# First products of every stage interleaved, and the residual, merged and last gate tiles turned by VectorE and DMA instead of TensorE

## The chip, the cores and the metric

The kernel runs on one core of a Trainium2 chip. The metric is the device time of one launch, in microseconds (us). Of three timed runs the median counts; beside them stands one profiled run, whose trace the rows below come from.

## What the kernel computes

One block of a network on 256 tokens of width 2048, in float32. Cut to what matters:

```python
h = rms_norm(x, ffn1_norm)
x = x + 0.5 * ((silu(h @ w1_gate) * (h @ w1_up)) @ w1_down)      # D_FF = 5632
h = rms_norm(x, mix_norm)
proj = h @ w_in                                                  # 2048 -> 3072
y_a = s5_mixer(proj[:, :1024], ...)                              # diagonal state space, then a GLU
y_b = sgu_mixer(proj[:, 1024:], ...)                             # gated by a 128-token mixing
g_a, g_b = split(sigmoid(h @ w_gate + b_gate))
merged = g_a * (y_a @ w_branch_a) + g_b * (y_b @ w_branch_b)
x = x + merged @ w_out
h = rms_norm(x, ffn2_norm)
x = x + 0.5 * ((silu(h @ w2_gate) * (h @ w2_up)) @ w2_down)
out = rms_norm(x, final_norm)
```

## The kernel before

Tokens are the rows of every result: 256 tokens are two halves of 128 partitions, and a result tile is 128 x 2 x 512 in PSUM (`acc`, three buffers). The weights stream once: chunks of 128 x 2048 floats (1 MB) come from HBM on SyncE's queue into `raw`, ScalarE rounds a chunk to `whi`, VectorE takes the rest as `wlo = raw - whi`, and each product is the sum of three matmuls (hi x whi, hi x wlo, lo x whi). A chunk holds four k-steps of 512 columns, and a **step** is six matmuls of 512 columns: three for each token half. `job(lhs, kt, evac)` runs kt steps into one `acc` and then queues `evac`, which reads the result.

The program is written out by one counter of steps (`tick`). Before each step a tick runs the functions that were put there with `at(delta, fn)`, then the waiting evacuations, and, at the first step of a chunk, the split of the chunk two further on; fillers (the preparation of the S5 mixer, for instance) get their turns by a credit per tick. Each engine runs what it got in this order.

The left operand of a product must have its contraction index on the partitions, so every result that feeds a later product is turned. There are two ways in the kernel:

- `turned`: eight TensorE transposes of 128 x 128 into two PSUM tiles `q`, then `put`, which splits them into hi and lo on ScalarE and VectorE.
- `turned_dma`: two VectorE transposes of 32 x 32 blocks (128 x 512 each) into a tile `tt`, four DMAs on GpSimd's queue to a DRAM tile `turn` in runs of 32 floats, one DMA back into `w`, and `put` a fixed number of steps after the evacuation.

In each of the two feed-forward stages the 11 gate tiles are made in groups of 4, 4 and 3 (`GROUPS`); each group's down product follows it, over 16, 16 and 12 steps a tile and four tiles of 512 columns. All gate tiles but a group's last go through `turned_dma`; the group's last, the four tiles of x after each of the first two residual sums (`residual`), and the four merged tiles (`ba_evac`) go through `turned`. A stage's first product needs the last tile of the stage before at its step 12 of 16 (8 of 12).

Of the kernel before, what the change touches and what calls it, by code (L numbers as in the profile page):

```python
# [18 lines left out]
P = 128  # L19
# [11 lines left out]
GROUPS = (4, 4, 3)  # L31
# [19 lines left out]
def kernel(  # L51
# [57 lines left out]
    def add_ffn(wg, wu, wd, first):  # L109
        j, d = 0, 0  # L110
        for n in GROUPS:
            for _ in range(n):
                if j == 0 and first is not None:
                    add(first)
                else:
                    i = j - (first is not None)
                    add(wg, 4 * i, 4)
                    add(wu, 4 * i, 4)
                j += 1
            add(wd, d, 4 * n)  # L120
            d += 4 * n

    add_ffn(w1g, w1u, w1d, w1s)
    add(w_in)
# [7 lines left out]
    add(w_out)  # L132
    add_ffn(w2g, w2u, w2d, None)
# [115 lines left out]
    def split_gain(dst, src, g, k):  # L249
        act.activation(out=dst[:, 0, :], in_=src, func=AF.Copy, scale=g[:, k:k + 1])  # L250
        dve.scalar_tensor_tensor(out=dst[:, 1, :], in0=src, scalar=g[:, k:k + 1],
                                 in1=f(dst[:, 0, :]), op0=ALU.mult, op1=ALU.subtract)
# [10 lines left out]
    def turned_dma(src, pl, put, wait):  # L263
        tt = tmp()
        for h in range(2):
            dve.transpose(out=tt[:, h, :], in_=src[:, h, :])  # L266
        d = dr.tile([4, 32, 2, 4, P], F32, tag="turn", name="turn", bufs=2)
        dv = d.rearrange("b j h k (a i) -> a j (h k) b i", a=4)
        for a in range(4):
            pool.dma_start(out=dv[a], in_=tt[32 * a:32 * a + 32].rearrange("j h (k b i) -> j (h k) b i", k=4, b=4))  # L270
        w = pl.tile([P, 2, 4, P], F32, tag="tw", name="w")
        pool.dma_start(out=w.rearrange("p h k t -> p (h k t)"), in_=d.rearrange("b j h k t -> (b j) (h k t)"))

        def arrived():
            for h in range(2):
                put(slice(h * P, h * P + P), w[:, h])
        at(wait, arrived)
# [36 lines left out]
    def residual(hT, g, scale):  # L314
        def make(m):
            def put(b, q):
                for i in range(2):
                    k = 4 * m + 2 * b + i
                    split_gain(hT[:, k], q[:, i, :], g, k)

            def evac(acc):
# [3 lines left out]
                at(2, lambda: turned(x_sb, m * N, put))  # L325
# [5 lines left out]
    def ffn(hT, gp, last_down, begin=None, rates=None):  # L331
# [8 lines left out]
        def up_evac(gt, j, n):  # L340
            def put(b, q):
                split2(gt[:, 4 * j + 2 * b:4 * j + 2 * b + 2], q)

            def evac(acc):
# [13 lines left out]
        for i, n in enumerate(GROUPS):  # L358
# [3 lines left out]
            for j in range(n):  # L362
                if begin is not None and i == 0 and j == 0:
                    begin(gate_evac, up_evac(gt, j, n))
# [3 lines left out]
            if i == len(GROUPS) - 1:  # L368
                last_down(gt, 4 * n)
            else:  # L370
                for m in range(4):
                    job(gt, 4 * n, down(m))
# [461 lines left out]
    def down_mix(gt, kt):  # L834
# [4 lines left out]
        for m in range(4):  # L839
            job(gt, kt, mk(m))  # L840

    ffn(h1, gp, down_mix, begin, (0.3, 0.35, 0.35))
# [24 lines left out]
    def load_bias(i):  # L867
        b = ev.tile([P, N], F32, tag="bias", name="bias", bufs=2)
# [53 lines left out]
    job(h2, KD, gelu_to(v, 0))  # L922
    job(h2, KD, gelu_to(v, 1))
# [118 lines left out]
    def ba_evac(n):  # L1042
        def put(b, q):
            split2(mT[:, 4 * n + 2 * b:4 * n + 2 * b + 2], q)
# [11 lines left out]
    for m in range(4):  # L1056
        job(mT, KD, lambda acc, m=m: later["mk"](m)(acc))
        if m == 0:
            mxr.release()
            mxa.release()  # L1060
            h3p = tc.alloc_tile_pool(name="h3p", bufs=1)
            h3 = h3p.tile([P, KD, 2, T], F32R, name="h3")
            later["mk"] = residual(h3, g3, 1.0)
    gp2 = tc.alloc_tile_pool(name="gp2", bufs=1)

    def down_out(gt, kt):
# [19 lines left out]
        for m in range(3):  # L1086
            job(gt, kt, evac(m))
# [27 lines left out]
    ffn(h3, gp2, down_out)  # L1115
# [8 lines left out]
def _layout(inputs):  # L1124
# [14 lines left out]
    def down(w):  # L1139
        parts, r = [], 0  # L1140
        for n in GROUPS:
# [7 lines left out]
    def pairs(a):  # L1149
# [20 lines left out]
        'w1s': start, 'w1g': wide(wg[:, N:]), 'w1u': wide(wu[:, N:]), 'w1d': down(i['ffn1_w_down'][0]),  # L1170
# [11 lines left out]
        'w2g': wide(i['ffn2_w_gate'][0]), 'w2u': wide(i['ffn2_w_up'][0]), 'w2d': down(i['ffn2_w_down'][0]),  # L1182
# [23 lines left out]
```

## Time and profile before

| | us |
|---|---|
| three timed runs | 2028.51, 2028.75, 2030.27 (median 2028.75) |
| the profiled run's own time | 2029.23 |
| its span, first to last instruction | 2027.3 |
| TensorE (PE) busy | 2008.8 (99%) |
| VectorE (DVE) busy | 1145.8 (57%) |
| ScalarE (ACT) busy | 864.4 (43%) |
| GpSimd (POOL) busy | 144.9 (7%) |
| mean granted TensorE clock | 0.997 |

Busy time of TensorE is counted from modelled ends: two matmuls that overlap count once, so a share of 99% says that it hardly ever stood still, not how fast it worked. What a matmul costs is read from the distance between the starts of neighbours.

### The profile page before, as it was taken

To read this page: it belongs to the slowest core of one execution; us is meant where nothing else is said; L and a number is where in the kernel's file an instruction comes from. 1 tells how busy PE (TensorE), PEld (TensorE's weight loads), DVE (VectorE), ACT (ScalarE), POOL (GpSimd) and SP (SyncE) were. 2 spreads that over 40 slices of the span, in tenths; PEclk is the share of its full clock that TensorE was granted. 3 is DMA by queue.
4 is the path that set the end of the run, shared out by engine and by line. 5 is a ranking of instruction groups with operands and counts; after the bars stand their busy time and mean duration, and the time that the engine had idled before them with its cause. 6 is when DMAs were issued, how large, how long until landed. Compare 5 with 4: busy or idle time off the path is not lost.

```text
span 2027.3 us, 23118 instructions
## 1 busy us (share of the span) xinstructions
PE 2008.8 (99%) x9636; PEld 1660.9 (82%) x9636; DVE 1145.8 (57%) x1138; ACT 864.4 (43%) x709; POOL 144.9 (7%) x214
## 2 busy tenths in 40 slices
PE   9999999999999999999999999999999999999998
PEld 7888888888888888878888988888888888888886
DVE  5775555666664555556775565544554445544454
ACT  7544334444334454434434544534433343333343
POOL 0111002221010000011100000000000000000100
PEclk9999999999999999999999999999999999999999
DMA  8667666765666556556765454566655666555653
GB/s 314 229 229 251 229 237 227 239 227 201 217 234 210 182 182 216 199 184 245 240 223 202 185 187 171 198 213 218 218 187 189 217 217 209 189 202 194 224 207 125
DMA packets 71865, 428.97 MB, mean 212 GB/s; under 512 B 11552, under 2 KB 12208, under 8 KB 25936
## 3 DMA queue, kind: packets, MB, share of 16 engines
q1 hardware_dynamic: 53280, 378.56, 52.8%
q0 software_dynamic: 16032, 44.71, 7.7%
q10 hardware_dynamic: 2448, 4.22, 0.6%
q8 instruction: 75, 1.23, 0.2%
q14 instruction: 30, 0.25, 0.0%
HBM read 406.60 MB, written 20.84 MB: 211 GB/s over the span
## 4 chain that ended last, share of the span: by engine, by line
PE 97%; DVE 1%; DMA 1%; ACT 1%; issue 1%; SPq 0%; ACTq 0%
PE acc L218 31%; PE acc L220 31%; PE acc L219 31%; PE q L260 1%; DMA raw<-in_w1s_dram 1%; ACT whi L148 0%; DVE wlo L149 0%; PE q L609 0%; PE acc L236 0%; PE acc L235 0%; PE acc L234 0%; PE q L745 0%; PE q L702 0%; DVE r L671 0%; PE acc L1099 0%
## 5 line engine op out<-in xcount | busy, mean ns | idle before, releaser
L149 DVE TENSOR_TENSOR wlo<-raw,whi 128x2048 fp32r<-128x2048 f32 (+1 forms) x363 | 815.3, 2248 | 772.6 <-ACT whi L148 772.6
L148 ACT ACTIVATE whi<-raw 128x2048 fp32r<-128x2048 f32 (+1 forms) x363 | 682.6, 1882 | 920.3 <-PE acc L220 853.7
L218 PE MATMUL acc<-whi,h 128*128 128x512 f32 x1856 | 725.9, 391 | 0.8 <-ACT whi L148 0.8
L219 PE MATMUL acc<-wlo,h 128*128 128x512 f32 x1856 | 723.2, 390 | 1.1 <-DVE wlo L149 1.1
L220 PE MATMUL acc<-whi,h 128*128 128x512 f32 x1856 | 722.7, 389 | 0.0
L218 PEld LDWEIGHTS acc<-whi,h 128*128 128x128 f32 x1856 | 348.8, 188 | 74.7 <-ACT whi L148 1.4
L219 PEld LDWEIGHTS acc<-wlo,h 128*128 128x128 f32 x1856 | 348.7, 188 | 73.9 <-DVE wlo L149 2.5
L220 PEld LDWEIGHTS acc<-whi,h 128*128 128x128 f32 x1856 | 348.6, 188 | 72.5
L218 PE MATMUL acc<-whi,gt 128*128 128x512 f32 x680 | 266.6, 392 | 0.0
L220 PE MATMUL acc<-whi,gt 128*128 128x512 f32 x680 | 265.9, 391 | 0.0
L219 PE MATMUL acc<-wlo,gt 128*128 128x512 f32 x680 | 264.8, 389 | 0.0
L220 PEld LDWEIGHTS acc<-whi,gt 128*128 128x128 f32 x680 | 127.7, 188 | 27.5
L219 PEld LDWEIGHTS acc<-wlo,gt 128*128 128x128 f32 x680 | 127.7, 188 | 27.4
L218 PEld LDWEIGHTS acc<-whi,gt 128*128 128x128 f32 x680 | 127.7, 188 | 26.4
L270 POOL DMA_DIRECT2D turn<-t x64 | 63.5, 999 | 931.2 <-DVE t L266 931.2
L337 ACT ACTIVATE t<-acc,rc 128x512 f32<-128x512 f32 x44 | 27.9, 685 | 63.4 <-PE acc L220 63.4
L218 PE MATMUL acc<-whi,mT 128*128 128x512 f32 x128 | 50.2, 392 | 0.0
L312 DVE SCALAR_TENSOR_TENSOR x_sb<-acc,x_sb 128x1024 f32<-128x1024 f32 x27 | 33.1, 1225 | 29.7 <-PE acc L220 29.7
L220 PE MATMUL acc<-whi,mT 128*128 128x512 f32 x128 | 49.8, 389 | 0.0
L219 PE MATMUL acc<-wlo,mT 128*128 128x512 f32 x128 | 49.8, 389 | 0.0
L291 ACT ACTIVATE junk<-x_sb 128x512 bf16<-128x512 f32 x32 | 20.2, 630 | 56.9 <-DVE x_sb L312 51.6
L347 DVE SCALAR_TENSOR_TENSOR t<-acc,rc,t 128x512 f32<-128x512 f32 x44 | 30.9, 745 | 16.8 <-PE acc L220 16.8
(205 smaller groups left out, 1086.3 us busy)
## 6 DMA issues: line engine op xcount, KB each, us to landing
raw<-in_w1d_dram SPq DMA_DIRECT2D x44, 1024.0 KB, 4.9
raw<-in_w2g_dram SPq DMA_DIRECT2D x44, 1024.0 KB, 4.8
raw<-in_w2u_dram SPq DMA_DIRECT2D x44, 1024.0 KB, 5.5
raw<-in_w2d_dram SPq DMA_DIRECT2D x44, 1024.0 KB, 4.8
raw<-in_w1g_dram SPq DMA_DIRECT2D x40, 1024.0 KB, 5.0
raw<-in_w1u_dram SPq DMA_DIRECT2D x40, 1024.0 KB, 5.9
raw<-in_w_in_dram SPq DMA_DIRECT2D x24, 1024.0 KB, 4.8
raw<-in_w_gb_dram SPq DMA_DIRECT2D x16, 1024.0 KB, 5.0
```

The lines of the kernel that those rows point to most:

```text
L148: act.activation(out=hi[:, s], in_=r[:, s], func=AF.Copy)
L149: dve.tensor_tensor(out=lo[:, s], in0=r[:, s], in1=f(hi[:, s]), op=ALU.subtract)
L218: pe.matmul(acc[:, h, :], lhsT=lhs[:, k, 0, t], rhs=hi, start=first, stop=False)
L219: pe.matmul(acc[:, h, :], lhsT=lhs[:, k, 0, t], rhs=lo, start=False, stop=False)
L220: pe.matmul(acc[:, h, :], lhsT=lhs[:, k, 1, t], rhs=hi, start=False, stop=last)
L260: pe.transpose(q[:, i, h * P:h * P + P], src[:, h, c:c + P], ident)
L270: pool.dma_start(out=dv[a], in_=tt[32 * a:32 * a + 32].rearrange("j h (k b i) -> j (h k) b i", k=4, b=4))
L291: act.activation(out=j, in_=x_sb[:, h, m * N:m * N + N], func=AF.Square, accum_out=ssq[:, h, m:m + 1])
L312: dve.scalar_tensor_tensor(out=xs, in0=acc, scalar=scale, in1=xs, op0=ALU.mult, op1=ALU.add)
L337: act.activation(out=s[:, h, :], in_=acc[:, h, :], func=AF.Silu, scale=rc(h))
L347: dve.scalar_tensor_tensor(out=s[:, h, :], in0=acc[:, h, :], scalar=rc(h), in1=s[:, h, :], op0=ALU.mult, op1=ALU.mult)
```

## The change

`braid` takes two or three products at once: it runs all but the last four steps of each, one product after the other, and then the last four steps of each. It is used for the first two products (three where they have 12 steps) of each down product, of `w_in`, of `w_out` and of the second feed-forward stage, and the weight chunks are put in the same order. A stage's last tile is so first needed at step 24. With that, the residual tiles, the merged tiles and the last gate tile of each group go through `turned_dma` too, with waits of 18, 16 and 17 steps; the other gate tiles wait 24 steps instead of 26. The tile `w` becomes two halves, each loaded by a DMA of its own, which share two buffers with the bias tiles. The residual's split works on pieces of 128 x 128 instead of 128 x 256. The first feed-forward stage's groups become 3, 4, 4. `turned` stays in two places, the SGU's tiles (`ub`) and the S5's input tiles (`ua_evac`).

```diff
-GROUPS = (4, 4, 3)
+GROUPS1 = (3, 4, 4)
+GROUPS2 = (4, 4, 3)
...
+    def braid(jobs, between=None):
+        accs = [new_acc() for _ in jobs]
+        for (lhs, kt, _), acc in zip(jobs, accs):
+            for k in range(kt - 4):
+                step(acc, lhs, k, k == 0, False)
+        if between:
+            between()
+        for (lhs, kt, evac), acc in zip(jobs, accs):
+            for k in range(kt - 4, kt):
+                step(acc, lhs, k, False, k == kt - 1)
+            pend.append(lambda evac=evac, acc=acc: evac(acc))
...
-        w = pl.tile([P, 2, 4, P], F32, tag="tw", name="w")
-        pool.dma_start(out=w.rearrange("p h k t -> p (h k t)"), in_=d.rearrange("b j h k t -> (b j) (h k t)"))
-
-        def arrived():
+        w = []
+        for h in range(2):
+            w.append(half_tile("w").rearrange("p (k t) -> p k t", k=4))
+            pool.dma_start(out=w[h].rearrange("p k t -> p (k t)"),
+                           in_=d[:, :, h].rearrange("b j k t -> (b j) (k t)"))
+        at(wait, lambda: put(w))
...
     def residual(hT, g, scale):
         def make(m):
-            def put(b, q):
-                for i in range(2):
-                    k = 4 * m + 2 * b + i
-                    split_gain(hT[:, k], q[:, i, :], g, k)
+            def put(w):
+                for i in range(4):
+                    k = 4 * m + i
+                    for h in range(2):
+                        split_gain(hT[:, k, :, h * P:h * P + P], w[h][:, i], g, k)
 
             def evac(acc):
                 add_residual(acc, m, scale)
                 for h in range(2):
                     square(m, h)
-                at(2, lambda: turned(x_sb, m * N, put))
+                turned_dma(x_sb[:, :, m * N:m * N + N], put, 18)
...
-                if j < n - 1:
-                    turned_dma(s, gp, lambda c, w: split2(gt[:, 4 * j:4 * j + 4], w, c), 26)
-                else:
-                    at(2, lambda: turned(s, 0, put))
+                turned_dma(s, split_turned(gt[:, 4 * j:4 * j + 4]), 24 if j < n - 1 else 17)
...
+    def downs(gt, kt, evacs):
+        b = strands(kt // 4)
+        braid([(gt, kt, e) for e in evacs[:b]])
+        for e in evacs[b:]:
+            job(gt, kt, e)
...
-    job(h2, KD, gelu_to(v, 0))
-    job(h2, KD, gelu_to(v, 1))
+    braid([(h2, KD, gelu_to(v, 0)), (h2, KD, gelu_to(v, 1))])
...
         def evac(acc):
-            t = tmp()
-            dve.tensor_tensor(out=t, in0=acc, in1=cols(ga, n), op=ALU.mult)
+            t = cols(ga, n)
+            dve.tensor_tensor(out=t, in0=acc, in1=t, op=ALU.mult)
             dve.tensor_tensor(out=t, in0=t, in1=cols(mb, n), op=ALU.add)
-            at(2, lambda: turned(t, 0, put))
+            turned_dma(t, split_turned(mT[:, 4 * n:4 * n + 4]), 16)
...
+    braid([(mT, KD, out_evac(m)) for m in range(2)], open_h3)
+    for m in (2, 3):
+        job(mT, KD, out_evac(m))
...
-        for m in range(3):
-            job(gt, kt, evac(m))
+        braid([(gt, kt, evac(m)) for m in range(3)])
```

What the change moves is shown at three places. The first is TensorE at the start of the output product `w_out`, whose left operand is the merged tile `mT`. Before, the last merged tile `t` is turned there, after the first two steps of the first product (`acc_8487`):

```order
L220 MATMUL acc_8487<-whi_8415,mT_8191 128x512
L260 MATMUL q_8509<-ident_80,t_8488 128x128 x4
L260 MATMUL q_8516<-ident_80,t_8488 128x128 x4
L218 MATMUL acc_8487<-whi_8415,mT_8191 128x512
L219 MATMUL acc_8487<-wlo_8416,mT_8191 128x512
```

With the change, after step 12 of the first product (`acc_8544`) the second product (`acc_8545`) begins, and no transpose stands among the steps:

```order
L237 MATMUL acc_8544<-whi_8566,mT_8253 128x512
L238 MATMUL acc_8544<-wlo_8567,mT_8253 128x512
L239 MATMUL acc_8544<-whi_8566,mT_8253 128x512
L237 MATMUL acc_8545<-whi_8596,mT_8253 128x512
L238 MATMUL acc_8545<-wlo_8597,mT_8253 128x512
L239 MATMUL acc_8545<-whi_8596,mT_8253 128x512
```

The eight transposes are gone from TensorE's row of work, and the four last steps of the first product stand behind twelve of the second.

The second place is VectorE at the same stage. Before, a merged tile is made (`t` from `acc` and the gate `ga`, plus `mb`), the next chunk's `wlo` follows, and then the split of the tile from PSUM (`q`):

```order
L1048 TENSOR_TENSOR t<-acc,ga 128x1024
L1049 TENSOR_TENSOR t<-t,mb 128x1024
L149 TENSOR_TENSOR wlo<-raw,whi 128x2048
L247 TENSOR_TENSOR mT<-q,mT 128x2x256 x2
L149 TENSOR_TENSOR wlo<-raw,whi 128x2048
```

With the change, from the second tile's making on: its block transposes, two chunks, the split of the first tile, and the start of the third tile's making:

```order
L1085 TENSOR_TENSOR ga<-acc,ga 128x2x512
L1086 TENSOR_TENSOR ga<-ga,mb 128x2x512
L300 STREAM_TRANSPOSE t<-ga 128x512 x2
L168 TENSOR_TENSOR wlo<-raw,whi 128x2048 x2
L278 TENSOR_TENSOR mT<-w,mT 128x4x128 x2
L1085 TENSOR_TENSOR ga<-acc,ga 128x2x512
```

Two block transposes a tile are new on VectorE; the split reads a tile `w` that a DMA brings, and stands four chunks behind its tile's making where it stood one behind.

The third place is ScalarE where the first feed-forward stage ends and `w_in` begins: `junk,ssq` are the squares of an x tile, `h` its split. Before:

```order
L291 ACTIVATE junk,ssq<-x_sb 128x512 x2
L148 ACTIVATE whi<-raw 128x2048
L250 ACTIVATE h_4783<-q,vec_sb 128x256 x4
L280 ACT_TABLE_LOAD
L280 ACTIVATE rc<-sm,eps_t 128x2
L148 ACTIVATE whi<-raw 128x2048 x3
```

With the change the last tile's split stands four chunks later, and the one before it lies where the last one's was:

```order
L330 ACTIVATE junk,ssq<-x_sb 128x512 x2
L167 ACTIVATE whi<-raw 128x2048
L281 ACTIVATE h_4683<-w,vec_sb 128x128 x8
L319 ACT_TABLE_LOAD
L319 ACTIVATE rc<-sm,eps_t 128x2
L167 ACTIVATE whi<-raw 128x2048 x4
L281 ACTIVATE h_4683<-w,vec_sb 128x128 x8
L167 ACTIVATE whi<-raw 128x2048 x2
```

Each split of `h` waits there for a DMA's tile `w`, with the following chunks' `whi` behind it in the same queue.

## Rows read from the trace of the kernel before

**Rows 1.** The page: busy time of each engine, and the chain of work that ended last, by engine and by line.

```profile
PE 2008.8 (99%) x9636; PEld 1660.9 (82%) x9636; DVE 1145.8 (57%) x1138; ACT 864.4 (43%) x709; POOL 144.9 (7%) x214
PE 97%; DVE 1%; DMA 1%; ACT 1%; issue 1%; SPq 0%; ACTq 0%
```

**Rows 2.** Who TensorE's matmuls waited for: line waited at, releaser, us in total, times, longest.

```profile
PE q L260 <- DVE u_all L934: 4.6, 1, 4.6
...
PE acc L219 <- DVE wlo L149: 1.1, 3, 0.6
```

**Rows 3.** The transposes of `turned` (L260), by what they read: count, and duration of one in ns (shortest, median, longest).

```profile
L260 PE MATMUL q<-ident,t x96: 270/273/446, 185.6 to 1955.8; 128*128 128x128 f32 x96
...
L260 PE MATMUL q<-ident,x_sb x64: 271/272/273, 695.2 to 1300.2; 128*128 128x128 f32 x64
```

**Rows 4.** TensorE in order of time around one call of `turned` on a residual tile, and then around one on a merged tile: start, us, instruction.

```profile
695.02 0.39 PE L220 MATMUL acc<-whi,gt 128*128 128x512 f32 x1
695.25 1.03 PE L260 MATMUL q<-ident,x_sb 128*128 128x128 f32 x8
696.04 0.48 PE L218 MATMUL acc<-whi,gt 128*128 128x512 f32 x1
...
696.82 0.39 PE L218 MATMUL acc<-whi,gt 128*128 128x512 f32 x1
...
1184.44 0.40 PE L220 MATMUL acc<-whi,yas 128*128 128x512 f32 x1
1184.75 1.06 PE L260 MATMUL q<-ident,t 128*128 128x128 f32 x8
1185.57 0.47 PE L218 MATMUL acc<-whi,yas 128*128 128x512 f32 x1
...
1186.34 0.39 PE L218 MATMUL acc<-whi,yas 128*128 128x512 f32 x1
```

**Rows 5.** ScalarE, then VectorE, in order of time over two chunks of the second feed-forward stage: splits of weights (L148, L149), the split of a gate tile that `turned_dma` brought (L246, L247), and the evacuation of the next one (L347, L266). In brackets the engine's idle time before, and what ended it.

```profile
1417.52 1.92 ACT L148 ACTIVATE whi<-raw 128x2048 fp32r<-128x2048 f32 x1 [3.52 <-PE acc L220]
1419.35 1.13 ACT L246 ACTIVATE gt<-w 128x512 fp32r<-128x512 f32 x2
1422.96 1.92 ACT L148 ACTIVATE whi<-raw 128x2048 fp32r<-128x2048 f32 x1 [2.48 <-PE acc L220]
...
1419.47 2.29 DVE L149 TENSOR_TENSOR wlo<-raw,whi 128x2048 fp32r<-128x2048 f32 x1 [3.15 <-ACT whi L148]
1421.68 1.29 DVE L247 TENSOR_TENSOR gt<-w,gt 128x512 fp32r<-128x512 f32 x2
...
1428.40 1.41 DVE L347 SCALAR_TENSOR_TENSOR t<-acc,rc,t 128x512 f32<-128x512 f32 x2 [1.20 <-PE acc L220]
1429.73 1.29 DVE L266 STREAM_TRANSPOSE t<-t 128x512 f32<-128x512 f32 x2
```

**Rows 6.** GpSimd's queue in order of time: the four issues to `turn` and the issue of `w`, for the call whose evacuation ends rows 5, for one late in the second feed-forward stage and for one early in the first. Below them the time from issue to landing of the DMAs of L270 and of L272 (shortest, median, longest).

```profile
1431.32 3.96 POOL L270 DMA_DIRECT2D turn<-t  x4 [32.96 <-DVE t L266]
...
1868.37 3.96 POOL L270 DMA_DIRECT2D turn<-t  x4 [164.02 <-DVE t L266]
1878.23 0.56 POOL L272 DMA_DIRECT2D w<-turn  x1 [5.90 <-DMA turn<-t]
...
100.13 3.95 POOL L270 DMA_DIRECT2D turn<-t  x4 [34.68 <-DVE t L266]
111.84 0.56 POOL L272 DMA_DIRECT2D w<-turn  x1 [7.76 <-DMA turn<-t]
...
DMA to landing us min/median/max: 3.3/5.8/8.1
...
DMA to landing us min/median/max: 3.6/4.3/7.2
```

**Rows 7.** VectorE in order of time: four splits of 128 x 128 pieces in the SGU (L913); and the first half of a merged tile's making (L1048). Then ScalarE's and VectorE's split of residual tiles as they are (128 x 256), grouped by line: count, busy us, mean ns of one.

```profile
838.08 1.12 DVE L913 SCALAR_TENSOR_TENSOR ub<-q,bs_sb,ub 128x128 f32<-128x128 f32 x4
...
1170.19 1.23 DVE L1048 TENSOR_TENSOR t<-acc,ga 128x1024 f32<-128x1024 f32 x1 [1.20 <-PE acc L220]
...
L251 DVE SCALAR_TENSOR_TENSOR h<-q,vec_sb,h 128x256 fp32r<-128x256 f32 x32 | 14.7, 480 | 8.7 <-ACT h L250 8.7
L250 ACT ACTIVATE h<-q,vec_sb 128x256 fp32r<-128x256 f32 x32 | 14.1, 467 | 23.8 <-DVE h L251 23.8
```

**Rows 8.** VectorE in order of time in the last down product: the evacuation of the second tile (L312, L1073) and the `wlo` behind it, then the same of the third tile, and the two results that end the kernel (L1102).

```profile
1986.06 1.22 DVE L312 SCALAR_TENSOR_TENSOR x_sb<-acc,x_sb 128x1024 f32<-128x1024 f32 x1 [1.20 <-PE acc L220]
1987.32 1.29 DVE L1073 TENSOR_TENSOR fin<-x_sb,fin 128x512 f32<-128x512 f32 x2
1990.70 2.29 DVE L149 TENSOR_TENSOR wlo<-raw,whi 128x2048 fp32r<-128x2048 f32 x1 [2.08 <-ACT whi L148]
...
2010.54 0.69 DVE L1102 SCALAR_TENSOR_TENSOR x_sb<-acc,x_sb 128x512 f32<-128x512 f32 x1 [1.46 <-PE acc L1100]
...
2018.70 0.69 DVE L1102 SCALAR_TENSOR_TENSOR x_sb<-acc,x_sb 128x512 f32<-128x512 f32 x1 [4.43 <-PE acc L1100]
```

**Rows 9.** TensorE in order of time behind its longest wait: two neighbouring matmuls there; and the stretch of 8 us about them (us, busy PE, PEld, DVE, ACT, POOL, granted clock, DMA share, GB/s).

```profile
869.42 0.63 PE L219 MATMUL acc<-wlo,h 128*128 128x512 f32 x1
869.85 0.63 PE L220 MATMUL acc<-whi,h 128*128 128x512 f32 x1
...
864.00:872.00 8.00, 5.94 (x20) 4.96 (x21) 3.80 (x12) 0.00 (x0) 1.47 (x2) 0.57 0.59 200
```

More of the change, by code (lines that the diff above doesn't have):

```diff
@@ L107, in add, with braided, strands, add_ffn @@
         chunks.extend(w[i] for i in range(a, w.shape[0] if n is None else a + n))
-    def add_ffn(wg, wu, wd, first):
+    def braided(w, a, n, jobs):
+        for i in range(jobs):
+            add(w, a + n * i, n - 1)
+        for i in range(jobs):
+            add(w, a + n * i + n - 1, 1)
+    def strands(n):
+        return 2 if n == 4 else 3
+    def add_ffn(wg, wu, wd, groups, first):
         j, d = 0, 0
-        for n in GROUPS:
+        for n in groups:
             for _ in range(n):
-                if j == 0 and first is not None:
+                i = j - (first is not None)
+                if i < 0:
                     add(first)
+                elif j == 0:
+                    add(wg, 0, 3)
+                    add(wu, 0, 3)
+                    add(wg, 3, 1)
+                    add(wu, 3, 1)
                 else:
-                    i = j - (first is not None)
                     add(wg, 4 * i, 4)
@@ L261, in turned, with half_tile, turned_dma @@
             put(b, q)
-    def turned_dma(src, pl, put, wait):
+    def half_tile(name):
+        return ev.tile([P, N], F32, tag="half", name=name, bufs=2)
+    def turned_dma(src, put, wait):
         tt = tmp()
@@ L329, in residual, with ffn @@
         return make
-    def ffn(hT, gp, last_down, begin=None, rates=None):
+    def ffn(hT, gp, groups, last_down, begin=None, rates=None):
         state = {}
@@ L356, in down @@
             return lambda acc: add_residual(acc, m, 0.5)
-        for i, n in enumerate(GROUPS):
+        for i, n in enumerate(groups):
             gt = gp.tile([P, 16, 2, T], F32R, tag="gt", name="gt")
@@ L362, in ffn @@
             for j in range(n):
-                if begin is not None and i == 0 and j == 0:
-                    begin(gate_evac, up_evac(gt, j, n))
+                if i == 0 and j == 0:
+                    if begin is not None:
+                        begin(gate_evac, up_evac(gt, j, n))
+                    else:
+                        braid([(hT, KD, gate_evac), (hT, KD, up_evac(gt, j, n))])
                     continue
@@ L367, in ffn @@
                 job(hT, KD, up_evac(gt, j, n))
-            if i == len(GROUPS) - 1:
+            if i == len(groups) - 1:
                 last_down(gt, 4 * n)
             else:
-                for m in range(4):
-                    job(gt, 4 * n, down(m))
+                downs(gt, 4 * n, [down(m) for m in range(4)])
+    def downs(gt, kt, evacs):
[3 more added lines that the diff above has]
+            job(gt, kt, e)
     stash_e = dr.tile([2, 2, 4, NPAIR, 64], F32, name="stash_e")
@@ L838, in down_mix @@
         mk = residual(h2, g2, 0.5)
-        for m in range(4):
-            job(gt, kt, mk(m))
-    ffn(h1, gp, down_mix, begin, (0.3, 0.35, 0.35))
+        downs(gt, kt, [mk(m) for m in range(4)])
+    ffn(h1, gp, GROUPS1, down_mix, begin, (0.3, 0.35, 0.35))
     gp.release()
@@ L867, in load_bias @@
     def load_bias(i):
-        b = ev.tile([P, N], F32, tag="bias", name="bias", bufs=2)
+        b = half_tile("bias")
         act.dma_start(out=b, in_=bgr[i:i + 1, :].to_broadcast([P, N]))
@@ L1055, with out_evac, open_h3 @@
     later = {}
[L1056 to L1063, printed above, removed]
+    def out_evac(m):
+        return lambda acc: later["mk"](m)(acc)
+    def open_h3():
+        mxr.release()
+        mxa.release()
+        later["p"] = tc.alloc_tile_pool(name="h3p", bufs=1)
+        later["h3"] = later["p"].tile([P, KD, 2, T], F32R, name="h3")
+        later["mk"] = residual(later["h3"], g3, 1.0)
+    braid([(mT, KD, out_evac(m)) for m in range(2)], open_h3)
+    for m in (2, 3):
+        job(mT, KD, out_evac(m))
+    h3p, h3 = later["p"], later["h3"]
     gp2 = tc.alloc_tile_pool(name="gp2", bufs=1)
@@ L1137, in cols, with down @@
         return a.reshape(-1, P).T
-    def down(w):
+    def down(w, groups):
         parts, r = [], 0
-        for n in GROUPS:
+        for n in groups:
             parts.append(wide(w[r:r + n * N]))
```

36 lines of the change are left out of this document (19 added, 17 removed).

## The prediction, made blind

> **What bounds the kernel now.** I read the busy times and the chain first: TensorE is busy 99% of the span and makes 97% of the chain that ended last [rows 1]. Busy time can hide waits, so the table of waits came next: the matmuls of the products waited for weights about a microsecond in all, and the one long wait, 4.6 us, is for an S5 input tile that the change leaves alone [rows 2]. Then the pace in the timeline: neighbours start 0.23 us apart [rows 4], so a step of six matmuls takes 1.37 us and a chunk of four 5.47 us. ScalarE shows the same from the other side: its splits start 5.44 us apart, and its idle time ends when TensorE gives a weight buffer back [rows 5]. TensorE sets the pace; whatever leaves its queue comes off the time, as long as nothing new makes it wait.
>
> **What is removed.** A call of `turned` has eight transposes; 64 on `x_sb` and 96 on `t` [rows 3] are 8 calls and 12. The 8 on x go, and of the 12 all but the two of `ua_evac`: 6 on gate tiles and 4 on merged tiles. Together 18 calls, 144 transposes. What a call costs is the place that it takes in TensorE's row. On an x tile, four starts of ordinary matmuls later than 695.02 would be 695.94 and was 696.82: 0.88 us. On a merged tile, four starts after 1184.44 would be 1185.36 and was 1186.34: 0.98 us [rows 4]. With 0.88 for x and gate tiles: 14 x 0.88 + 4 x 0.98 = 16.2 us.
>
> The transposes' own durations say something else: 144 x 272 ns = 39.2 us [rows 3]. The Trainium skill ("TensorE: Matmul & The Clock Gate", part 4 on the PE-mode transpose) gives about 275 ns for such a transpose in a kernel's context; the trace agrees on the duration. By it the sum would be 39.6 us and the time 1989. But eight of them fill 1.03 us in the row, not 2.2 [rows 4]: they overlap, and the place taken counts.
>
> The reordering itself (braids, groups 3, 4, 4) adds and removes no matmul: nothing. It needs two or three `acc` at once, of three: the third is the last up tile's, read out at the braid's start and used 16 steps later.
>
> **What is added, and what hides it.** Per call: two block transposes on VectorE, 1.29 us [rows 5], about 6 us of GpSimd's issuing, and three DMA legs. In a chunk of 5.47 us VectorE has 2.29 us of `wlo`, ScalarE 1.92 of `whi` [rows 5]; both have room. A split of weights is done 4.24 us after its buffer comes free (1417.52 to 1421.76 [rows 5]) and is used two chunks, 10.9 us, later: 6.7 us of cover. This is what hides everything that is put in front of a split; gone, each us late costs TensorE one.
>
> The question is whether the tiles arrive. From the evacuation's start to the first issue on GpSimd it is 2.9 us [rows 5, 6]; from there to the issue of `w` 9.9 us, 11.7 in the slowest call shown; to the landing 4.3 (3.6 to 7.2) [rows 6]. Together 17.1 us, at most 21.8; the second half of `w` follows 0.56 us later. The waits are 16, 17, 18 and 24 steps: 21.9, 23.3, 24.7, 32.9 us. So `put` finds its tile there, and step 24, where the last tile of a stage is first read, is 32.9 us after its evacuation. Gate and x tiles: 0 us of stall.
>
> Three places are tighter.
>
> (a) *Two x tiles four steps apart.* Braided evacuations follow each other at 4 steps, and there are two halves of `w` only: GpSimd holds the second tile's `w` until the first tile's split has read its own. In the last down product of the first stage, with evacuations at steps 28 and 32, the first split is emitted at 46 and done at about 49 (16 pieces: on VectorE 8 x 0.28 = 2.2 us [rows 7]; on ScalarE no more than 8 x 0.467 = 3.7 [rows 7]). The second `w` is issued then and lands some 5 us later, near step 52.5. The second split stands at step 50, so ScalarE waits there and is free at about 54.5; the weights due at 52 are done by 57.6 instead of 55 and needed at 60. 3.3 us of cover are left: 0. With the slowest landing (7.2) 0.4 us are left: still 0.
>
> (b) *Merged tiles.* They come every 8 steps (10.96 us), with 16 steps' wait, and GpSimd needs 9.9 to 11.7 us from the first issue to `w`, plus 1.1 for its two issues. From the stage's start in us: tile 0 is ready to issue at 10.96 + 2 x 1.23 [rows 7] + 1.6 = 15.0, its `w` goes out at 25.3 (10.3, between the two calls) and lands at 29.6. Tile 1 follows on GpSimd at 26.4, `w` 36.7; tile 2 at 37.8, `w` 48.1, landed 52.4 and 53.0. VectorE ends the `wlo` before it at 53.6 and splits tile 2 by 54.9. The output product's first product reads it at its step 8, which is step 40 here: 54.8. Just in time: between 0 and, with 11.7 and 7.2 all along (`w` of tile 2 out at 52.3, landed 59.5 and 60.1), about 5.3 us of stall. I take 0.3, since the rows' usual times lie at that end.
>
> (c) *The end.* The last down product now has evacuations at steps 28, 32 and 36. Each keeps the next `wlo` back: 1986.06 to 1992.99, 6.9 us [rows 8] against 5.47 for a chunk. After two in a row `wlo` is done 13.9 us after step 28; the chunk is read 12 matmuls after step 36, at 13.7. Stall 0 to 0.3 us; I take 0.2. The third evacuation ends at 18.6, before the first half of the last tile at 19.1 (the halves end 8.16 us apart [rows 8]).
>
> S5's preparation gets 147 turns instead of 150 before the drain and ends before it; its places move, for which I allow 0, within 1 us either way.
>
> **The sum.** -16.2 + 0.3 + 0.2 = -15.7 us. The profiled run, 2029.23 us, would become 2013.5; it lies 0.48 above the median, so the median 2028.75 becomes **2013.0 us**.
>
> **The rivals.**
>
> *Merged tiles late* (b at its upper end). 5.3 us of stall, and a wait of that length has a price of its own: behind the wait of 4.6 us the granted clock's mean was 0.57, the lower level of 1.2 GHz, and matmuls started 0.43 us apart instead of 0.23, six of them: 1.2 us [rows 9]. 2013.0 - 0.3 + 6.5 = 2019.2. For it: GpSimd takes 11.0 to 12.8 us per tile and they come every 10.96. Against: no `w` came later than 21.8 us.
>
> *Slower: the splits wait for tiles at every place.* ScalarE works in order, and behind each `put` stand weights. If the way through DRAM took longer than wait plus cover less the split's own work (about 1.1 us for gate and merged tiles, 2.4 for x), that is 28.9, 27.5 and 29.0 us, each of the 18 calls would stop TensorE. The gain is eaten where 6(L - 28.9) + 4(L - 27.5) + 8(L - 29.0) = 16.2: at L = 29.5 us; at 32 it is 60.6 us of stalls and 2073. Against: 16 calls of before show 17 to 22 us, under the same stream of weights. The Trainium skill speaks for it: "VectorE: DVE Perf Modes", on the three transpose paths and the rules for authors, would have a 128 x 128 transpose done by TensorE where PSUM will do, and calls a plain strided DMA copy 19 times slower than the DMA transpose (1.31 us): an estimate from it is 25 us a block, eight to a call. No run here shows that: the trace has a whole call, 32 x 32 blocks already turned by VectorE, at about 17 us.
>
> *No change: TensorE's place is filled by waits.* If weights were the limit, the gaps would stay and the time with them, 2028.7. Against: a microsecond of waits for weights in the whole span [rows 2], ScalarE idle 3.5 us before each split [rows 5].
>
> **How the numbers follow.** Gain of 14 to 18 us: 0.80. Late merged tiles or several small stalls, 2015 to 2020: 0.13. No change: 0.03. Slower: 0.04. The likeliest case alone is 2011 to 2015: up to 0.2 us more a call and S5's 1 us below, the small stalls doubled above. The range, 2011 to 2019, takes in most of the second case. A change of 0.2%, 4 us, is about what a measurement of this kernel can tell from none; faster by more 0.93, within it 0.03, slower 0.04.
>
> **What would show it.** Right: transposes on `t` and `x_sb` down to 16, starts 0.23 us apart across the places where they were, no new releaser among TensorE's waits, `w` landing 16 to 22 us after the evacuation. (a) wrong: ScalarE's split `h<-w` in the waits with many us and `acc` waiting for `whi` or `wlo` behind it. (b) wrong: a wait of TensorE for `mT` at step 8 of the output product, and a stretch at half clock. (c) wrong: a wait for `wlo` in the last 25 us. The prediction fails if `w` takes more than 27 us, or if the long wait at the S5 input grows or goes.

## The result, and the profile after

The changed kernel takes 2014.57 us (median of four runs, 2013.46 to 2018.92), the kernel before 2028.63 beside it (four runs, 2028.26 to 2030.27): a ratio of 0.9933, 95% interval 0.9918 to 0.9948. That is 14.1 us less, where 15.7 were forecast (2013.0, range 2011 to 2019). The profiled run took 2014.35 us with a span of 2012.6, against 2027.3 before.

The page of the changed kernel, busy time and the chain that ended last, as in [rows 1]:

```profile
PE 1992.8 (99%) x9492; PEld 1646.2 (82%) x9492; DVE 1170.9 (58%) x1206; ACT 870.1 (43%) x741; POOL 245.2 (12%) x338
PE 95%; DMA 2%; DVE 1%; ACT 1%; issue 0%; POOL 0%; SPq 0%; ACTq 0%; POOLq 0%; DVEq 0%
```

TensorE has the 144 instructions less and still makes nearly the whole chain. GpSimd is busy 100 us more and VectorE 25 more, and they make no more than 1% of the chain each. What is left of the transposes on `t`, to be read beside [rows 3] (busy us, mean ns, then idle time before them and its cause):

```profile
L291 PE MATMUL q<-ident,t 128*128 128x128 f32 x16 | 2.9, 318 | 4.6 <-DVE u_all L974 4.6
```

The operand `x_sb` is gone and `t` is down from 96 to 16; the 16 transposes on the SGU's `ub`, which the change leaves alone, stay. TensorE's waits after, as in [rows 2] (us in total, times, longest):

```profile
PE q L291 <- DVE u_all L974: 4.6, 1, 4.6
...
PE q L948 <- DVE u_all L974: 1.2, 1, 1.2
PE acc L237 <- ACT mT L277: 1.2, 1, 1.2
```

The long wait at the S5 input is what it was. One releaser is new: `mT`, the merged tile. TensorE in order of time at that place, step 8 of the output product's first product, and below it ScalarE's split of the tile for which it waits:

```profile
1206.62 0.39 PE L239 MATMUL acc<-whi,mT 128*128 128x512 f32 x1
1208.19 0.50 PE L237 MATMUL acc<-whi,mT 128*128 128x512 f32 x1 [1.19 <-ACT mT L277]
...
1208.92 0.50 PE L239 MATMUL acc<-whi,mT 128*128 128x512 f32 x1
1209.54 0.50 PE L237 MATMUL acc<-whi,mT 128*128 128x512 f32 x1
...
1210.61 0.40 PE L237 MATMUL acc<-whi,mT 128*128 128x512 f32 x1
...
1207.51 0.63 ACT L277 ACTIVATE mT<-w 128x512 fp32r<-128x512 f32 x1 [3.99 <-DMA w<-turn]
1208.86 0.63 ACT L277 ACTIVATE mT<-w 128x512 fp32r<-128x512 f32 x1 [0.72 <-DMA w<-turn]
```

From 1206.62 to 1210.61 there are seven distances, 3.99 us; at the usual 0.23 they would be 1.60. So this place costs 2.4 us, the wait of 1.19 and the pieces about it, and ScalarE had stood still for the DMA of `w`. Why the tile is late shows in GpSimd's queue: the merged stage, then the first residual tiles of the stage behind it (an issue of four DMAs to `turn`, then the two of `w`; in brackets what GpSimd waited for):

```profile
1167.32 4.10 POOL L304 DMA_DIRECT2D turn<-t  x4 [103.35 <-DVE t L300]
1179.13 1.11 POOL L308 DMA_DIRECT2D w<-turn  x2 [7.71 <-DMA turn<-t]
1180.22 3.98 POOL L304 DMA_DIRECT2D turn<-t  x4
1192.17 1.10 POOL L308 DMA_DIRECT2D w<-turn  x2 [7.97 <-DMA turn<-t]
1193.27 3.99 POOL L304 DMA_DIRECT2D turn<-t  x4
1204.31 1.11 POOL L308 DMA_DIRECT2D w<-turn  x2 [7.05 <-DMA turn<-t]
...
1239.54 3.98 POOL L304 DMA_DIRECT2D turn<-t  x4 [21.66 <-DVE t L300]
1248.05 1.11 POOL L308 DMA_DIRECT2D w<-turn  x2 [4.54 <-DMA turn<-t]
1249.14 3.98 POOL L304 DMA_DIRECT2D turn<-t  x4
1264.82 1.10 POOL L308 DMA_DIRECT2D w<-turn  x2 [11.70 <-DVE h L282]
```

In the merged stage it is 11.8, 12.0 and 11.0 us from the first issue to that of `w`; the residual tile at 1239.54 needs 8.5 (the one behind it is held on purpose, until the first split has read its half of `w`). With 1.1 us for the issue of `w`, a tile takes GpSimd 12.7 us on the mean of these three, and the tiles come every 10.96: each stands in the queue for longer than the one before, and the third is the one TensorE waits for.

### The profile page after: what moved, and what is told of

It is laid out like the page before. It is cut to its first block, busy times and chain, and to the rows that moved or that the text cites. A ratio compares the mean times of both kernels' runs of the same rounds, so it can differ in the third digit from the quotient of the medians.

```text
span 2012.6 us, 23202 instructions
## 1 busy us (share of the span) xinstructions
PE 1992.8 (99%) x9492; PEld 1646.2 (82%) x9492; DVE 1170.9 (58%) x1206; ACT 870.1 (43%) x741; POOL 245.2 (12%) x338
## 3 DMA queue, kind: packets, MB, share of 16 engines
q0 software_dynamic: 22624, 63.59, 11.2%
## 4 chain that ended last, share of the span: by engine, by line
PE 95%; DMA 2%; DVE 1%; ACT 1%; issue 0%; POOL 0%; SPq 0%; ACTq 0%; POOLq 0%; DVEq 0%
PE acc L237 31%; PE acc L238 30%; PE acc L239 30%; DMA turn<-t 1%; DMA raw<-in_w1s_dram 1%; ACT whi L167 0%; PE q L651 0%; PE acc L267 0%; PE acc L266 0%; PE acc L265 0%; PE q L787 0%; PE q L744 0%; POOL turn L304 0%; PE acc L1142 0%; PE acc L1143 0%
## 5 line engine op out<-in xcount | busy, mean ns | idle before, releaser
L304 POOL DMA_DIRECT2D turn<-t x136 | 135.4, 1002 | 926.0 <-DVE t L300 892.4
L308 POOL DMA_DIRECT2D w<-turn x68 | 37.6, 557 | 219.3 <-DMA turn<-t 154.2
```

The costliest lines, as they stand in the source:

```text
L308: pool.dma_start(out=w[h].rearrange("p k t -> p (k t)"), in_=d[:, :, h].rearrange("b j k t -> (b j) (k t)"))
```

## The experiments

In the expectations, theory A is the prediction's accounting (a call of `turned` costs its place in TensorE's row, the order nothing, the merged stall 2.4 us), B holds that the new order is what pays, and C that a call costs its transposes' durations.

### The order alone

All three kinds of tile are turned by TensorE again; order, braids and groups stay as changed. The edit in its core (it puts the edits of the next three experiments together):

```diff
-                turned_dma(x_sb[:, :, m * N:m * N + N], put, 18)
+                at(2, lambda: turned(x_sb, m * N, put))
...
-            turned_dma(t, split_turned(mT[:, 4 * n:4 * n + 4]), 16)
+            at(2, lambda: turned(t, 0, lambda b, q: split2(mT[:, 4 * n + 2 * b:4 * n + 2 * b + 2], q)))
```

> The new order alone: braids, groups 3-4-4, split halves of w stay; the residual, merged and last gate tiles are turned by TensorE again. Theory A (the gain is the place that the 18 calls take in TensorE's row; the order itself is worth nothing): 2028.6 us plus the 0.3 us that the last three evacuations cost, so 2028 to 2030, and 176 transposes in the trace. Theory B (the gain comes from the order, the transposes were hidden): near 2014.6. Theory C (each transpose costs its own 272 ns): as A here.

Measured: 2034.51 us (2033.05 to 2035.87) against 2028.86, ratio 1.0022 (1.0013 to 1.0032). B is out: the order by itself gains nothing. A is off as well, since the order by itself costs 5.7 us. The waits of this kernel have the reason, then TensorE and VectorE in order of time at the first of the two places:

```profile
PE q L291 <- DVE x_sb L351: 3.7, 2, 1.9
...
701.73 0.40 PE L239 MATMUL acc<-whi,gt 128*128 128x512 f32 x1
703.92 1.09 PE L291 MATMUL q<-ident,x_sb 128*128 128x128 f32 x8 [1.80 <-DVE x_sb L351]
704.77 0.48 PE L237 MATMUL acc<-whi,gt 128*128 128x512 f32 x1
...
702.25 0.48 DVE L282 SCALAR_TENSOR_TENSOR h<-q,vec_sb,h 128x256 fp32r<-128x256 f32 x1 [0.54 <-ACT h L281]
702.65 1.21 DVE L351 SCALAR_TENSOR_TENSOR x_sb<-acc,x_sb 128x1024 f32<-128x1024 f32 x1
```

In a braid two x tiles end four steps apart. VectorE is still in the split of the first, piece by piece in turn with ScalarE (`<-ACT h`), when the second `acc` is ready; it makes the second x tile only at 702.65, and TensorE's transposes, placed two steps after the evacuation, wait for it. From 701.73 to 704.77 is one ordinary distance and 2.8 us, where a call takes about 0.8 at the same reading of [rows 4] (695.02 to 696.04). Two such places are 4.0 us of the 5.7; the spans of the two profiled executions differ by 4.5 (2031.8 and 2027.3), and the rest was not placed. With `turned_dma` no engine but GpSimd waits for the tile, so in the changed kernel this wait does not exist.

### Merged tiles by TensorE

```diff
-            t = cols(ga, n)
-            dve.tensor_tensor(out=t, in0=acc, in1=t, op=ALU.mult)
+            t = tmp()
+            dve.tensor_tensor(out=t, in0=acc, in1=cols(ga, n), op=ALU.mult)
...
-            turned_dma(t, split_turned(mT[:, 4 * n:4 * n + 4]), 16)
+            at(2, lambda: turned(t, 0, lambda b, q: split2(mT[:, 4 * n + 2 * b:4 * n + 2 * b + 2], q)))
```

> The changed kernel with the four merged tiles alone turned by TensorE again. A: 4 x 0.98 us come back, the 2.4 us of waiting for mT go: 2014.6 + 3.9 - 2.4 = 2016.1 us. B: only the waiting goes, 2012.2. C: 4 x 2.2 us come back, 2014.6 + 8.7 - 2.4 = 2020.9.

Measured: 2015.71 us (2015.42 to 2016.03), ratio 0.9931 (0.9917 to 0.9946); no wait for `mT` in its trace. A's 2016.1 holds. Four calls back and the stall away nearly cancel: of the 3.9 us that this part was to give, 2.4 go in the stall. The traces say so more sharply than the medians. This kernel and the changed one run the same matmuls of the products in the same order, so the two traces can be laid side by side, matmul by matmul: in the merged stage this one falls 4.0 us behind (four calls), and at step 8 of the output product it gets 2.4 back. By the times alone it can't be said whether the merged tiles' part pays at all, since the changed kernel by itself varies by 5 us (see below).

### Residual tiles by TensorE

```diff
-                turned_dma(x_sb[:, :, m * N:m * N + N], put, 18)
+                at(2, lambda: turned(x_sb, m * N, put))
```

> The changed kernel with the eight tiles of x alone turned by TensorE again. A: 8 x 0.88 us come back: 2014.6 + 7.0 = 2021.6 us. B: 2014.6. C: 8 x 2.2: 2032.

Measured: 2025.78 us (2024.92 to 2030.3), ratio 0.9987 (0.9978 to 0.9996), 11.2 us above the changed kernel and 4.2 above A's 2021.6. Eight calls at 0.88 are 7.0; the other 4.2 are the wait met above, with the same row in its waits (`x_sb`, 3.7 us, twice, longest 1.9). In its trace the eight calls with the two waits take 11.2 us, read as in [rows 4]. C's 2032 would have been 17.4 above. So the x tiles' part of the change is worth 11 us given the braid, though only 7 of them were there before it.

### Last gate tiles by TensorE

```diff
-                turned_dma(s, split_turned(gt[:, 4 * j:4 * j + 4]), 24 if j < n - 1 else 17)
+                if j < n - 1:
+                    turned_dma(s, split_turned(gt[:, 4 * j:4 * j + 4]), 24)
+                else:
+                    at(2, lambda: turned(s, 0, lambda b, q: split2(gt[:, 4 * j + 2 * b:4 * j + 2 * b + 2], q)))
```

> The changed kernel with the last gate tile of each of the six groups turned by TensorE again. A: 6 x 0.88 us come back: 2014.6 + 5.3 = 2019.9 us. B: 2014.6. C: 6 x 2.2: 2027.7.

Measured: 2020.67 us (2020.25 to 2021.56), ratio 0.9955 (0.9939 to 0.9972): 6.1 above the changed kernel; A's 5.3 is nearest. In its trace the six calls take 5.3 us, read as in [rows 4], which is A's sum; the rest is in waits of that execution (for `mT` 2.6 us where the changed kernel's profiled one has 1.2). All three parts thus price a call by its place in the row, not by its duration.

### The changed kernel again

No edit: five more executions of the changed kernel, for the spread.

> The changed kernel itself, beside the next three on one chip: 2014 to 2015 us, and again about 2.4 us lost by TensorE at step 8 of the output product.

Measured: 2017.99 us (2014.23 to 2019.38) against 2029.43, ratio 0.994 (0.9927 to 0.9954). The expected 2014 to 2015 was missed. This kernel spreads over 5 us, the one before, beside it, over 1.5 (in the nineteen executions beside the runs above, over 2.5, but for one of 2036.97). The profiled execution, of 2017.99, at the same step 8, and the 8 us about it (us, busy PE, PEld, DVE, ACT, POOL, granted clock, DMA share, GB/s):

```profile
1208.35 0.39 PE L239 MATMUL acc<-whi,mT 128*128 128x512 f32 x1
1210.14 0.50 PE L237 MATMUL acc<-whi,mT 128*128 128x512 f32 x1 [1.40 <-ACT mT L277]
...
1211.96 0.80 PE L237 MATMUL acc<-whi,mT 128*128 128x512 f32 x1 [0.59 <-ACT mT L277]
1212.55 0.63 PE L238 MATMUL acc<-wlo,mT 128*128 128x512 f32 x1
1212.98 0.63 PE L239 MATMUL acc<-whi,mT 128*128 128x512 f32 x1
...
1215.11 0.43 PE L238 MATMUL acc<-wlo,mT 128*128 128x512 f32 x1
1215.38 0.39 PE L239 MATMUL acc<-whi,mT 128*128 128x512 f32 x1
...
1208.00:1216.00 8.00, 6.01 (x18) 3.96 (x17) 5.50 (x4) 3.06 (x3) 3.37 (x4) 0.79 0.97 325
```

Two waits, 1.40 and 0.59, and then starts 0.43 us apart until 1215.11: the clock fell to 1.2 GHz, which it did not in the execution shown above (1.00 over the same 8 us). The place costs 4.3 us here (1208.35 to 1215.38, twelve distances of 0.23 taken off) instead of 2.4. That is 1.9 of the 3.6 us by which the two spans differ (2016.2 and 2012.6). Side by side, matmul by matmul, the rest lies at two places: 0.8 us in the first 20 us of the kernel, and 0.9 behind the S5 wait, where the granted clock over 8 us is 0.50 here and 0.60 there, and 0.94 and 1.00 in the next 8.

### The output product's braid leaves eight steps

The last eight steps of each of the two products are put last there, and `w_out`'s chunks ordered to match; the third merged tile is first read 8 steps later.

```diff
-    braided(w_out, 0, 4, 2)
+    braided(w_out, 0, 4, 2, 2)
...
-            for k in range(kt - 4):
+            for k in range(kt - last):
...
-    braid([(mT, KD, out_evac(m)) for m in range(2)], open_h3)
+    braid([(mT, KD, out_evac(m)) for m in range(2)], open_h3, 8)
```

> The output product's braid puts the last eight steps of its first two products last in place of the last four, so that the third merged tile is first read at step 16 of the stage and not at step 8. If the 2.4 us are the lateness of that tile alone: 2.4 us less than the changed kernel, 2012.2, and no wait for mT. If the tile is only where a general lack of something shows (weights, ScalarE), the wait moves elsewhere and the time stays 2014.6.

Measured: 2013.41 us (2012.82 to 2015.11), ratio 0.9922 (0.991 to 0.9935); the changed kernel beside it had 2017.99. What is left of the wait in question:

```profile
PE acc L237 <- ACT mT L277: 0.6, 1, 0.6
```

The tiles come as slowly as before (11.1 to 12.1 us from first issue to `w`) and TensorE hardly notices. Five executions of this kernel lie within 2.3 us, five of the changed one beside it within 5.2.

### The merged tiles' writes on SyncE's queue

The four DMAs to `turn` are issued by SyncE instead of GpSimd, for the merged tiles alone. Theories: GpSimd's one queue makes the tiles late (Q), or the DMA engines, which the weights share, do (D).

```diff
-            pool.dma_start(out=dv[a], in_=tt[32 * a:32 * a + 32].rearrange("j h (k b i) -> j (h k) b i", k=4, b=4))
+            (out_q or pool).dma_start(out=dv[a], in_=tt[32 * a:32 * a + 32].rearrange("j h (k b i) -> j (h k) b i", k=4, b=4))
...
-            turned_dma(t, split_turned(mT[:, 4 * n:4 * n + 4]), 16)
+            turned_dma(t, split_turned(mT[:, 4 * n:4 * n + 4]), 16, nc.sync)
```

> For the merged tiles alone, SyncE's queue issues the four DMAs to DRAM; GpSimd issues the loads of w as before. Theory Q (GpSimd's one queue makes the tile late: four issues of 1 us, and each tile's issues behind the w of the tile before): the tile comes some 4 us earlier, no wait for mT, 2012.2 us. Theory D (the transfers are slow in this stage, whoever issues them, because the 128-byte runs share the DMA engines with w and the weights): the time from issue to landing stays as long and the wait stays, 2014.6.

Measured: 2014.39 us (2013.09 to 2016.32), ratio 0.9927 (0.9914 to 0.9939). SyncE's and GpSimd's issues for the first tile, one of ScalarE's splits of weights, and TensorE's wait:

```profile
1166.62 3.60 SPq L304 DMA_DIRECT2D turn<-t  x4
1170.32 1.43 SPq L162 DMA_DIRECT2D raw<-in_w_ba_dram  x2
...
1173.53 1.13 POOL L308 DMA_DIRECT2D w<-turn  x2 [110.06 <-DMA turn<-t]
...
1211.55 1.92 ACT L167 ACTIVATE whi<-raw 128x2048 fp32r<-128x2048 f32 x1 [5.17 <-DMA raw<-in_w_out_dram]
...
PE acc L239 <- DVE mT L278: 1.3, 1, 1.3
```

The first tile needs 6.9 us from issue to `w` instead of 11.8. But the weight loads now stand behind the writes in SyncE's queue, and ScalarE waits for weights, 5.2 us in the row shown. The third tile's `w` goes out at 1195.58, where it was 1204.31; but ScalarE and VectorE, held up before it by the weights, split it at 1205.24 and 1207.58 only, and TensorE still waits 1.3 us for a merged tile. This run does not part Q from D: while the writes go, the loads are held back too.

### The merged stage without weight loads

The 24 loads of `w_ba`'s and `w_out`'s chunks are left out; the splits read a tile of x instead, so the two products are of other numbers, and the work of TensorE, ScalarE, VectorE and GpSimd stays.

```diff
+            if BARE[0] <= j < BARE[1]:
+                raws[j] = x_sb[:, 0, :]
+            else:
+                t = wp.tile([P, SUB], F32, tag="raw", name="raw", bufs=NRAW)
+                nc.sync.dma_start(out=t, in_=chunks[j])
+                raws[j] = t
```

> The changed kernel without the 24 weight loads of w_ba and w_out: their splits read a tile of x instead, so the two products are of other numbers, with the same instructions on TensorE, ScalarE, VectorE and GpSimd. Theory Q (GpSimd's queue and its issues make the merged tiles late): from the first issue to w still 11 to 12 us, and the wait for mT stays. Theory D (the writes to DRAM share the DMA engines with the weights' loads): from the first issue to w 7 to 8 us, no wait for mT, 2.4 us or more off.

Measured: 2012.57 us (one run), and no wait for `mT`. GpSimd's queue in the merged stage, to be read beside that of the changed kernel:

```profile
1167.86 4.09 POOL L308 DMA_DIRECT2D turn<-t  x4 [103.38 <-DVE t L304]
1175.03 1.11 POOL L312 DMA_DIRECT2D w<-turn  x2 [3.08 <-DMA turn<-t]
1178.85 3.98 POOL L308 DMA_DIRECT2D turn<-t  x4 [2.71 <-DVE t L304]
```

The same queue, the same four issues of 4 us; but from the first issue to `w` it is 7.2 us (7.0 to 7.7 over the four tiles) instead of 11 to 12, and GpSimd waits for the second tile (`<-DVE t`) instead of the tile for GpSimd. Side by side with the changed kernel's trace, TensorE gets 2.4 us back at step 8 of the output product, as D said; the span is 1.9 shorter, since other places differ by half a microsecond (behind the S5 wait the granted clock is below 1 for longer here, 0.52 and 0.60 over the same 8 us). What D says of the weights is shown: the writes are slow because weights move at the same time, 4 to 5 us on a way of 7. GpSimd's one queue has its part in that it carries each tile's delay on to the next. The Trainium skill has a rule ("DMA: Bandwidth & Descriptors", on issuing engines not being separate DMA queues): transfers of all queues end up on the same 16 engines and interleave. The two traces agree in so far as loads issued by SyncE slow writes issued by GpSimd; whether they meet in these engines or in the memory behind them no run here tells.

### Residual tiles read four steps after their evacuation

The rival that ends on the other side, made to happen: the x tiles' `put` is placed where no tile can have come yet.

```diff
-                turned_dma(x_sb[:, :, m * N:m * N + N], put, 18)
+                turned_dma(x_sb[:, :, m * N:m * N + N], put, 4)
```

> The changed kernel with the split of an x tile put 4 steps behind its evacuation and not 18, so that ScalarE and VectorE stand before a tile that has not come, with weights behind it. By the prediction's cover (a late split costs what exceeds 6.7 us): a tile is split some 17 us after its evacuation, a chunk's weights due at 5.5 are ready at 21 and needed at 16.4, so about 5 us a tile and more for the second of a pair, 40 to 60 us in all, 2055 to 2075. If each us of ScalarE's waiting cost one: 8 x 11.5 us, 2107. If its spare time (43% busy) absorbed it: 2014.6.

Measured: 2090.28 us (one run) against 2028.86. TensorE's waits; ScalarE's first wait for an x tile; and a stretch of 70 us in each of the two residual stages (us, busy PE, PEld, DVE, ACT, POOL, granted clock, DMA share, GB/s):

```profile
PE acc L237 <- ACT whi L167: 40.8, 9, 9.0
PE acc L238 <- DVE wlo L168: 14.4, 11, 1.8
...
704.93 0.40 ACT L281 ACTIVATE h<-w,vec_sb 128x128 fp32r<-128x128 f32 x1 [10.28 <-DMA w<-turn]
...
690.00:760.00 70.00, 51.43 (x197) 39.99 (x196) 31.91 (x41) 28.12 (x45) 15.27 (x18) 0.87 0.49 151
1300.00:1370.00 70.00, 56.70 (x216) 44.48 (x215) 31.76 (x38) 24.91 (x40) 13.03 (x16) 0.87 0.56 179
```

This is the prediction's mechanism: ScalarE stops at `h<-w`, the weights' splits stand behind it, and TensorE waits for `whi` and `wlo`, 55.2 us where the changed kernel has 1.9. The 53 us more are the 40 to 60 expected; over eight tiles that is 6.7 us each, of 10.6 that ScalarE stands still (84.8 us in all). But the time rose by 75.7 us, past the 2055 to 2075 that were expected. The other 22 go with the clock, whose mean over the span is 0.982 instead of 0.997 and which is low in these same stretches: in 72 places neighbours start 0.40 to 0.46 us apart, where the changed kernel has four, and that makes 14 of the 22. The other 8 lie about the waits and were not taken apart.

### Both stalls taken away

The output product as above, and the first S5 input tile's transposes placed four steps after its evacuation instead of one.

```diff
-            at(1, lambda: turned(t, 0, put))
+            at(4 - 3 * n, lambda: turned(t, 0, put))
```

> The output product's braid with the last eight steps last, and the first S5 input tile's transposes four steps after its evacuation in place of one, so that VectorE has done the wlo that its copies stood behind. The trace has 4.6 + 1.2 us of waiting there, and 1.2 us of half clock behind it. If the half clock follows the wait: 2012.2 - 7.0 = 2005 us and a granted clock of 1.00 in the 8 us behind. If the lower clock comes from something else there: 2006.4, with the stretch still below 1. If the waiting moves on to the SGU's tiles, which share the two PSUM buffers: 2012.

Measured: 2004.48 us (2003.67 to 2005.76), ratio 0.9878 (0.9864 to 0.9891): faster than both kernels. The wait for `u_all` is gone; the stretch behind it, first in the changed kernel's trace:

```profile
858.00:866.00 8.00, 6.71 (x25) 5.60 (x26) 3.10 (x10) 0.00 (x0) 1.46 (x2) 0.60 0.57 198
```

and then in this one's:

```profile
858.00:866.00 8.00, 7.42 (x37) 6.04 (x37) 5.27 (x10) 2.45 (x2) 1.46 (x2) 1.00 0.80 252
```

From the kernel with the eight-step braid to this one it is 8.9 us in the medians, while the waits removed are 5.8 (4.6 and 1.2). Side by side, the two profiled executions differ by 7.5 us at this place, 1.7 more than the waits. The work at half clock behind them is gone, and the granted clock there is 1.00 now. What it cost shows in the eight-step kernel's trace, in two sets of eight matmuls of the SGU, one ahead of the wait and one behind it:

```profile
848.86 1.16 PE L948 MATMUL q<-v,ws_sb 128*128 128x128 f32 x8
...
860.22 2.05 PE L948 MATMUL q<-v,ws_sb 128*128 128x128 f32 x8 [1.21 <-DVE u_all L974]
```

The other 1.4 us of the medians were found in no trace.

## Why the prediction was right, point by point

**What is removed (16.2 us): right, half a microsecond too little.** Read at all 18 places of the trace before as in [rows 4], with 0.227 us for a start, the six gate calls take 5.6 us, the eight on x 7.1 and the four merged ones 4.0, together 16.7. The runs that give them back agree: 5.3 for the six, 7.2 for the eight once their waits are taken off, 4.0 for the four. A sum by the transposes' durations, 39.6, was wrong by 23. The rule that it came with, to leave a 128 x 128 transpose to TensorE (the Trainium skill, "VectorE: DVE Perf Modes", rules for authors), doesn't hold here: TensorE sets the pace, and giving the x tiles back to it costs 11.2 us, 7 of them for the transposes.

**The reordering (0): right for the changed kernel, by itself not free.** It costs 5.7 us as long as TensorE turns the x tiles. The prediction never looked at this pair; it made no difference to the sum, but it means that the two halves of the change do not add.

**(a) Two x tiles four steps apart (0): right.** The second tile's `w` does go out late, 15.7 us after its first issue, held by VectorE's split `h` as forecast. The forecast let ScalarE wait for it, some 3 us within the cover; in fact ScalarE reaches neither split too early: in the trace both follow a weights' split directly, and all of its waits for an x tile's `w` together are 0.4 us.

**(b) Merged tiles (0.3): right in place and kind, wrong in size.** It was forecast at step 8 of the output product, as a wait for `mT` through a late `w`, and that is where it is. It measured 2.4 us, 4.3 where the clock fell. The step that failed is the 10.3 us from the first issue to `w`: it came from the rows of calls elsewhere [rows 6], and in this stage it is 11.0 to 12.0. The rows had shown 11.7 for one call, and the text took it for the slow end; it is the ordinary case here. By the forecast's own clock, which has the first tile ready at 15.0, the third tile's `w` went out at 52.0, its slow end (52.3), and not at 48.1. That the weight loads make it so, the run without them shows; why they weigh more in this stage than in others was not tried (the 28 other calls of the changed kernel's trace that no split of an earlier tile holds back need 8.1 to 12.5 us beside the same stream, half of them less than 10). The landing of `w` was no part of the error: the third tile's halves went out at 1204.31 and 0.56 later, and ScalarE had them at 1207.51 and 1208.86, 3.2 and 4.0 us. With the slow end's 7.2 there it would have been the 5.3 us of stall; so it stayed at 2.4.

**(c) The end (0.2): right.** Two evacuations in a row keep back the `wlo`s as forecast. VectorE at the end of the changed kernel, to be read beside [rows 8]:

```profile
1976.52 1.23 DVE L351 SCALAR_TENSOR_TENSOR x_sb<-acc,x_sb 128x1024 f32<-128x1024 f32 x1 [1.20 <-PE acc L239]
...
1983.30 1.22 DVE L351 SCALAR_TENSOR_TENSOR x_sb<-acc,x_sb 128x1024 f32<-128x1024 f32 x1
...
1987.93 4.49 DVE L168 TENSOR_TENSOR wlo<-raw,whi 128x2048 fp32r<-128x2048 f32 x2 [2.08 <-ACT whi L167]
...
1995.84 0.69 DVE L1145 SCALAR_TENSOR_TENSOR x_sb<-acc,x_sb 128x512 f32<-128x512 f32 x1 [0.95 <-PE acc L1143]
...
2004.00 0.69 DVE L1145 SCALAR_TENSOR_TENSOR x_sb<-acc,x_sb 128x512 f32<-128x512 f32 x1 [4.44 <-PE acc L1143]
```

The evacuations are 6.8 us apart (forecast 6.9), and the first of the two `wlo` at 1987.93 is done at half of its 4.49 us, 13.7 us after the first evacuation's start (forecast 13.9). TensorE's starts there lose 0.24 us, and the halves still end 8.16 us apart.

**The sum.** With what was measured, -16.7, +2.4 and +0.2 are -14.1. The span of the profiled execution fell by 14.7: 0.2 of the difference lies in the first 20 us, the rest was not placed. So two terms of the forecast were off, 0.5 and 2.1 us in opposite senses, and that the first median came within 1.6 us of 2013.0 is in part luck. Over all nine executions of the changed kernel the median is 2016.4, and one, 2019.38, lies above the range.

**The rivals.** *Merged tiles late* is what happens in part: 2.4 us in one traced execution and 4.3, with the half clock that it foresaw, in the other, of its 6.5. Three of the nine executions (2018.92, 2018.96, 2019.38) are near its 2019.2, and the second median, 2017.99, is in its case; no trace of those three was kept, so that they are this rival is not shown. It had 0.13; what spoke against it, that no `w` had come later than 21.8 us, was read from stages other than its own. *Slower* happens only when the waits are cut, at the price that the run with four steps shows, and more, since it left out the clock. *No change* is out.

## What to carry to other kernels

Price an instruction on the pacing engine by the distance between its neighbours' starts, and a DMA round trip by rows of the stage where it will run, or, if it has none yet, by the slow end of the others, not by the kernel's median: with or without the weights' stream, the way from the first write's issue to `w` took 12 or 7 us. Where results are made to end close together, look at who makes them and who waits for the second; a consumer that can wait on a queue of its own takes that cost away. Count a wait of TensorE dearer than its length, since the clock may fall behind it. And where two kernels run the same matmuls in the same order, lay their traces side by side: that told 2.4 us from a spread of 5.

## What the runs showed of the hardware that was not expected

- A wait of about 1.2 us left the clock at 2.4 GHz in one execution of a kernel; 1.4 and 0.6 us in a row, with a few matmuls between, were followed by matmuls 0.43 us apart (1.2 GHz) in another execution of the same kernel. Longer waits did not always do that: with the last gate tiles on TensorE it waited 1.5 and 1.1 us for `mT`, and the granted clock over the 8 us about them was 1.00. So the length of a wait does not by itself say here whether the clock falls. Of the 3.6 us between the two traced executions of the changed kernel, 1.9 lie at that place.
- SyncE took 3.1 to 5.0 us for the issue of the four writes to `turn`, hardly less than GpSimd's 4.0, and loads queued behind them came late.
